# Emitting the conv of unit 20 and four weight tiles of the first down product inside the last up pair, and activation loads ahead of weight loads

## The chip, the cores and the metric

The kernel runs on one core of a Trainium2 chip. The metric is the device time of one execution in microseconds (us). A time without further words is the median of three runs; the profile is one execution more, with a time of its own.

## The reference, cut to what matters

One decoder layer: a mixer (retention and spatial gating), then a gated MLP with a causal depthwise convolution of width 3, then a last norm. The change lies wholly in the MLP, of which this is the computation (sequence 1024, model width 1024, inner width 2816, float32):

```
h = rmsnorm(x, ffn_norm_g[l])
up = causal_depthwise_conv(h @ w_up[l], conv_w[l], conv_b[l])
a, b = jnp.split(up, 2, axis=-1)
x = x + (jax.nn.silu(a) * b) @ w_down[l]
...
return rmsnorm(x, final_norm_g)
```

## The kernel before, in words

**Arithmetic.** Both matrix products of the MLP are done on 2x2 blocks with seven block products in place of eight (numbered 1 to 7). TensorE (PE) gets each float32 operand as two parts, a rounded one (h) and the rest (l): ScalarE (ACT) makes h by a copy, VectorE (DVE) makes l by a subtraction (`split_w`, L113 and L114, for weights; `load_act`, L809 and L810, for activations). Each block product then takes three matmuls for each pair of tiles: weight h with activation h, weight h with activation l, weight l with activation h. A matmul has 128 rows and 512 columns.

**Up units.** The inner width is cut into 22 tiles (FT = 22); one `Unit` computes a tile of both halves of the up product (`u20`, `u21` are the last two). Its steps on PE come in the order 1, 2, 5, 6, 3, 7, 4. Their weights: `a` and `d` are parts of the loaded tiles; `s` (split into `bh`, `bl`; steps 5 and 6) and `t` (split into `ch`, `cl`; steps 3 and 7) are sums of them, made on DVE in most units and, in the last pair, on GpSimd (POOL), L159. A unit's results `ra` and `rb` go to `conv`: `taps` for each of the two (ACT L756, DVE L757 and L758), a Silu (ACT L765) and the product of both (L767); the tiles are `cv20` and `cv42` for unit 20, `cv21` and `cv43` for unit 21. `blocks_of` then writes the products' activation blocks to memory (POOL: DMAs L774, L775, L778, L779 and subtractions L777), from where the down stage loads them.

**The last pair.** Unit 20 (`held`) is written out as the others, unit 21 (`last`) by `pair`, which calls a hook `ahead(1)` to `ahead(6)` between the steps; the hook emits first work of the down stage.

**The down stage.** Its seven products come in the order 2, 1, 5, 6, 3, 7, 4 (`SEQ`). A product has 4 output parts (p = 0 to 3) and 11 pairs of inner tiles, 33 matmuls for each part, 132 in all. Names: `wd20h` is the h part of weight tile 0 of product 2, with 8 of its 44 inner tiles, `g23l` the l part of activation tile 3 of product 2, with 2 of 11; so part p = 0 needs all activation tiles but of the weights only tiles 0 and 1. A product thus loads six weight tiles (512 KB each; two loads where two weights are summed) and six activation tiles (`g..`; the last of products 2 and 1 stays on chip as `g2e`, `g1e`). `dZ` are the sums of product 2 on PE, `dX` those of products 1, 6, 7 and 4, `dY` those of 5 and 3. `acc` (L855) adds finished sums to the output tiles `x2`.

**What sets the order.** The loads are issued by SyncE (SP), which works down its queue in order: a load that waits for its buffer holds all behind it. `PREP` is the list of a product's loads, and `prep(i, n)` emits the next n of product i. Raw up weights, their sums `s` and `t` and raw down weights share one pool of 4 tiles (`W`), so a load of a weight waits until the l part of the tile that had its place is made. The program's text does not fix the order on an engine: a scheduler sets it by due times and priorities as the text gives them, and each engine then works its own queue in order. In the down loop the order on PE is that of the text.

Of the kernel before, what the change touches and what calls it, by code (L numbers as in the profile page):

```python
# [13 lines left out]
ALU = mybir.AluOpType  # L14
# [9 lines left out]
FT = FF // P  # L24
# [41 lines left out]
def decoder_layer(ctx, tc, io, out):  # L66
    nc = tc.nc
# [8 lines left out]
    def U(name, dt=F32, shape=(P, 1024)):  # L76
        return up.tile(list(shape), dt, tag="u", name=name)
# [10 lines left out]
    def W(name):  # L88
        return wp.tile([P, 8, P], F32, tag="w", name=name, bufs=4)
# [16 lines left out]
    def split_w(src, name, tile=None, eng=None):  # L106
        n = src.shape[1]
        if tile:
            wh, wl = tile(name + "h"), tile(name + "l")
        else:  # L110
            wh = wp.tile([P, 8, P], F32R, tag="wh", name=name + "h")
            wl = wp.tile([P, 8, P], F32R, tag="wl", name=name + "l")
        nc.scalar.activation(wh[:, :n], src, AF.Copy)  # L113
        (eng or nc.vector).tensor_tensor(wl[:, :n], src, wh[:, :n].bitcast(F32), ALU.subtract)  # L114
        return wh, wl
# [35 lines left out]
    class Unit:  # L151
# [9 lines left out]
        def prep(u, src, key, eng=None):  # L161
            h, l = split_w(src, u.name + key, eng=eng)
            return [(h[:, o:o + u.kh], l[:, o:o + u.kh]) for o in range(0, src.shape[1], u.kh)]
# [105 lines left out]
    def unit(srcs, R, name):  # L269
        u = Unit(load_pair(srcs, name), R, name)  # L270
        u.prep_a()
        u.p(1)
        u.p(2)
        return finish(u)
# [479 lines left out]
    def taps(r, i):  # L754
        t = U(f"cv{i}")
        nc.scalar.activation(t, r, AF.Identity, scale=V("cw", 88 + i), bias=V("cb", i))  # L756
        nc.vector.scalar_tensor_tensor(t[:, 1:], r[:, :S - 1], V("cw", 44 + i), t[:, 1:], ALU.mult, ALU.add)  # L757
        nc.vector.scalar_tensor_tensor(t[:, 2:], r[:, :S - 2], V("cw", i), t[:, 2:], ALU.mult, ALU.add)  # L758
        return t
# [3 lines left out]
    def conv(ra, rb, i):  # L763
        a = taps(ra, i)
        nc.scalar.activation(a, a, AF.Silu)  # L765
        b = taps(rb, FT + i)
        (nc.gpsimd if i < 2 or i == FT - 2 else nc.vector).tensor_tensor(a, a, b, ALU.mult)  # L767
        g[i] = halves(a)


# [42 lines left out]
    def last_act(i, x):  # L813
        e = U(f"g{i}e", F32R, PAIR)
        nc.scalar.activation(e[:, 0], x, AF.Copy)
        nc.vector.tensor_tensor(e[:, 1], x, e[:, 0].bitcast(F32), ALU.subtract)
        act[i].append((e[:, 0], e[:, 1]))


    def load_wt(i, t):  # L820
        lo, n = 8 * t, min(8, NB - 8 * t)
        raw = []
        for m, src in enumerate(SRC[i]):
            raw.append(W(f"wd{i}{t}{m}")[:, :n])
            nc.sync.dma_start(raw[-1], src[:, lo:lo + n])
        w = raw[0]
        if i == 5:
            sums[t] = U(f"ds{t}", F32, (P, 8, P))
        if i in (5, 6, 3):
            s = sums[t][:, :n]  # L830
            x, y, op = {5: (w, raw[-1], ALU.add), 6: (s, w, ALU.subtract), 3: (w, s, ALU.subtract)}[i]
            nc.vector.tensor_tensor(s, x, y, op)  # L832
            w = s
        elif i == 7:
            nc.vector.tensor_tensor(w, w, raw[1], ALU.subtract)  # L835
        h, l = split_w(w, f"wd{i}{t}", tile=(lambda name: U(name, F32R, (P, 8, P))) if i == 2 and t % 2 == 0 or i == SEQ[-1] and t < 4 else None)
        wts[i] += [(h[:, m], l[:, m]) for m in range(n)]
# [3 lines left out]
    def load_x2(n):  # L841
        x2[n] = U(f"x2{n}")
        nc.sync.dma_start(x2[n], x2d[:, n])
# [12 lines left out]

    PREP = {2: [(load_act, j) for j in range(5)]}
    for i in SEQ[1:]:
        PREP[i] = [f for j in range(6) for f in ((load_act, j), (load_wt, j))]
        if i == 1:  # L860
            PREP[i] = [f for f in PREP[i] if f != (load_act, 5)]

# [6 lines left out]
    def pair(u, ahead):  # L869
        u.p(1)  # L870
        ahead(1)
        u.p(2)
        u.sums_s(nc.gpsimd)
        u.split_s()
        ahead(2)
        u.p(5)
        ahead(3)
        u.p(6)
        u.sums_t(nc.gpsimd)
        u.split_t()  # L880
        ahead(4)
        u.p(3)
        u.prep_b()
        ahead(5)
        u.p(7)
        ahead(6)
        u.p(4)

    for i, (ra, rb) in enumerate(early):
        conv(ra, rb, i)  # L890
    blocks_of(0)
    conv(*finish(u2), 2)
    for i in range(3, FT - 2):
        conv(*unit([io["w_up"][:, i], io["w_up"][:, FT + i]], R, f"u{i}"), i)
        if i % 2:
            blocks_of(i // 2)

    held = unit([io["w_up"][:, FT - 2], io["w_up"][:, 2 * FT - 2]], R, f"u{FT - 2}")
    last = Up(FT - 1)

    def ahead(j):
        if j in (1, 2, 3, 4, 5):
            prep(2, 1)
        if j == 4:
            load_wt(2, 0)
        if j == 5:
            load_wt(2, 1)
        if j == 6:
            prep(1, 1)

    pair(last, ahead)
    load_wt(2, 2)
    conv(*held, FT - 2)
    prep(1, 1)
    load_x2(0)
    load_x2(2)
    conv(last.ra, last.rb, FT - 1)
    e, o = g[FT - 2], g[FT - 1]
    last_act(2, o[:, 0])
    for t in range(3, 6):  # L920
        load_wt(2, t)
    last1 = U("g1e", F32R, PAIR)
    nc.scalar.activation(last1[:, 0], e[:, 0], AF.Copy)
    nc.vector.tensor_tensor(last1[:, 1], e[:, 0], last1[:, 0].bitcast(F32), ALU.subtract)
# [57 lines left out]
    with tc.manual_schedule(engines={mybir.EngineType.PE, mybir.EngineType.DVE, mybir.EngineType.Activation}):  # L982
# [8 lines left out]
        for k in range(8):  # L991
            s, p = divmod(k, 4)
            b = (bb, bc)[s]
# [54 lines left out]
```

## Time and profile before

| | before |
|---|---|
| median of 3 runs | 1091.77 us |
| lowest, highest | 1091.1, 1093.42 us |
| the profiled execution | 1095.39 us |
| its span on the core | 1093.6 us (so 1.8 us outside of it) |
| mean granted clock of TensorE | 0.978 |
| PE, DVE, ACT, POOL busy | 95%, 76%, 45%, 20% of the span |

Times in the rows are in us from the span's start. A row of a timeline gives the start, the duration, the engine, the line, what is written from what, and in brackets the idle time just before it with the instruction that ended it. Matmul durations overlap; their pitch, not their duration, says how fast PE goes. The last up unit ends and the down stage begins about 838 us after the start; product 4 ends just ahead of the end of the span.

### The profile page before, as it was taken

Reading aid. Unit: us, or ns where it says so; the run is one execution under the profiler, and the core shown is the slowest. Engines: PE = TensorE matmul, PEld = TensorE weight load, DVE = VectorE, ACT = ScalarE, POOL = GpSimd, SP = SyncE. Lnnn points to the kernel's source line nnn. Section 1 sums busy time; section 2 is a strip of 40 time slices with the busy share of each in tenths; the row PEclk is TensorE's granted clock in tenths of the full one; section 3 lists DMA queues with packets and bytes.
Section 4 is the critical chain, followed back from the end, with each engine's and each line's share of the span. In section 5 each row is a group of like instructions: output and inputs, shape, how many; then the busy total and the mean of one; then the engine's idle time right before and its main releaser. Section 6 shows DMA issues by size and latency. Waiting matters only on the chain.

```text
span 1093.6 us, 12687 instructions
## 1 busy us (share of the span) xinstructions
PE 1039.0 (95%) x4786; PEld 854.1 (78%) x4786; DVE 831.5 (76%) x990; ACT 492.3 (45%) x691; POOL 223.3 (20%) x152
## 2 busy tenths in 40 slices
PE   7798999999999997989999999999999979999986
PEld 5576888888888885778888888888887757888886
DVE  6967886968787398798887878788787747876655
ACT  6663434344455253553444544454454423344430
POOL 4502230513110006052223032122322210000000
PEclk9998999999999998999999999999999989999998
DMA  7251031212274240023333133232327568972514
GB/s 280 78 193 39 22 109 59 71 57 79 78 251 173 77 173 1 20 87 106 106 116 108 67 125 116 84 109 103 105 82 259 201 222 308 355 253 104 189 62 154
DMA packets 48445, 141.57 MB, mean 129 GB/s; under 512 B 5056, under 2 KB 9536, under 8 KB 48384
## 3 DMA queue, kind: packets, MB, share of 16 engines
q1 hardware_dynamic: 42752, 120.58, 31.8%
q0 software_dynamic: 5632, 20.19, 4.8%
q8 instruction: 37, 0.61, 0.2%
q14 instruction: 24, 0.20, 0.1%
HBM read 109.03 MB, written 31.72 MB: 129 GB/s over the span
## 4 chain that ended last, share of the span: by engine, by line
PE 67%; DVE 15%; issue 5%; DMA 4%; ACT 3%; POOL 1%; SPq 0%; DVEq 0%; ACTq 0%
PE dX L850 8%; PE po L135 8%; PE dY L850 5%; DVE cv L758 2%; DVE cv L757 1%; PE A2X L146 1%; PE G1X L146 1%; DMA g13l<-gb 1%; PE A3X L146 1%; PE B3X L146 1%; PE B1X L146 1%; PE u20X L146 1%; PE u0X L146 1%; PE G2X L146 1%; PE G3X L146 1%
## 5 line engine op out<-in xcount | busy, mean ns | idle before, releaser
L765 ACT ACTIVATE cv<-cv 128x1024 f32<-128x1024 f32 x22 | 23.4, 1062 | 71.8 <-DVE cv L758 71.8
L777 POOL TENSOR_TENSOR cv<-cv 128x512 f32<-128x512 f32 x22 | 38.4, 1745 | 22.1 <-DMA gb<-cv 16.5
L775 POOL DMA_DIRECT2D gb<-cv x11 | 7.9, 714 | 123.4 <-DVE cv L767 123.1
L777 POOL TENSOR_TENSOR cv<-cv,cv 128x512 f32<-128x512 f32 x22 | 29.6, 1346 | 4.2 <-DMA gb<-cv 2.4
L774 POOL DMA_DIRECT2D gb<-cv x11 | 6.5, 591 | 101.7 <-DVE cv L767 101.1
L936 ACT ACTIVATE x3q<-x 128x256 f32<-128x256 f32 (+1 forms) x21 | 9.4, 481 | 38.7 <-DVE x L997 30.2
L652 DVE TENSOR_TENSOR xr<-po,xr 128x512 f32<-128x512 f32 x16 | 10.9, 689 | 20.3 <-PE po L135 20.3
L675 POOL TENSOR_TENSOR nx<-nx,rsb 128x1024 f32<-128x1024 f32 x2 | 5.7, 2893 | 93.6 <-ACT rsb L719 93.6
L767 POOL TENSOR_TENSOR cv<-cv,cv 128x1024 f32<-128x1024 f32 x3 | 9.8, 3271 | 66.0 <-DVE cv L758 64.8
L767 DVE TENSOR_TENSOR cv<-cv,cv 128x1024 f32<-128x1024 f32 x19 | 23.1, 1217 | 0.1
L658 ACT ACTIVATE xq<-xr 128x512 f32<-128x512 f32 x14 | 8.8, 626 | 22.2 <-DVE xr L652 15.2
L546 ACT ACTIVATE sT<-po 128x128 f32<-128x128 f32 x32 | 8.4, 277 | 13.3 <-PE po L538 13.2
L832 DVE TENSOR_TENSOR ds<-wd,wd 128x1024 f32<-128x1024 f32 (+1 forms) x6 | 6.8, 1133 | 9.0 <-DMA wd<-in_w_down 9.0
L835 DVE TENSOR_TENSOR wd<-wd,wd 128x1024 f32<-128x1024 f32 (+1 forms) x6 | 6.8, 1135 | 8.6 <-DMA wd<-in_w_down 8.6
L284 POOL TENSOR_TENSOR nx<-nx,nx 128x1024 f32<-128x1024 f32 x4 | 12.3, 3093 | 3.5 <-DVE nx L729 3.5
L938 DVE TENSOR_TENSOR sq<-sq,x3q 128x256 f32<-128x256 f32 (+1 forms) x20 | 9.8, 517 | 4.2 <-ACT x3q L936 3.8
L947 DVE SCALAR_TENSOR_TENSOR x<-x,vec,r 128x256 f32<-128x256 f32 (+1 forms) x24 | 12.0, 565 | 0.8 <-PE r L619 0.8
L662 DVE TENSOR_TENSOR sq<-sq,xq 128x512 f32<-128x512 f32 x14 | 9.6, 688 | 2.5 <-ACT xq L658 2.3
L997 DVE TENSOR_TENSOR x<-dX,x 128x256 f32<-128x256 f32 x8 | 3.4, 424 | 9.8 <-PE dX L850 9.8
L672 ACT ACTIVATE nx<-xr,vec 128x512 f32<-128x512 f32 x16 | 10.8, 708 | 0.0
L509 ACT ACTIVATE kn<-pk,vec 128x512 f32<-128x512 f32 x8 | 5.2, 679 | 11.8 <-PE pk L508 11.8
L336 POOL TENSOR_SCALAR x<-x,vec 128x512 f32<-128x512 f32 x4 | 8.5, 2128 | 6.7 <-DVE R110l L330 6.7
(5707 smaller groups left out, 3893.5 us busy)
## 6 DMA issues: line engine op xcount, KB each, us to landing
wd<-in_w_down SPq DMA_DIRECT2D x45, 512.0 KB, 4.4
gb<-cv POOLq DMA_DIRECT2D x33, 512.0 KB, 3.2
wo<-in_w_out SPq DMA_DIRECT2D x10, 512.0 KB, 3.9
x<-in_xT SPq DMA_DIRECT2D x8, 512.0 KB, 9.2
xn<-in_xN SPq DMA_DIRECT2D x8, 512.0 KB, 6.0
xr<-in_xT SPq DMA_DIRECT2D x8, 512.0 KB, 6.1
x2d<-xr SPq DMA_DIRECT2D x8, 512.0 KB, 3.1
x<-x2d SPq DMA_DIRECT2D x8, 512.0 KB, 6.1
```

Of the source, the lines that this page charges most:

```text
L135: nc.tensor.matmul(ps, a, b, start=(k == 0 and t == 0), stop=(k == n - 1 and t == 2))
L146: nc.tensor.matmul(ps, a[:, k], b, start=(start and i == 0), stop=(i == 3 * n - 1), skip_group_check=not start)
L284: eng.tensor_tensor(o[j], a[j], b[j], ALU.subtract)
L652: nc.vector.tensor_tensor(u.y, u.ps, u.y, ALU.add)
L672: nc.scalar.activation(nx[n // 2][:, n % 2], xr[th][n // 2][:, n % 2], AF.Identity, scale=V("g2", n))
L757: nc.vector.scalar_tensor_tensor(t[:, 1:], r[:, :S - 1], V("cw", 44 + i), t[:, 1:], ALU.mult, ALU.add)
L758: nc.vector.scalar_tensor_tensor(t[:, 2:], r[:, :S - 2], V("cw", i), t[:, 2:], ALU.mult, ALU.add)
L765: nc.scalar.activation(a, a, AF.Silu)
L767: (nc.gpsimd if i < 2 or i == FT - 2 else nc.vector).tensor_tensor(a, a, b, ALU.mult)
L777: nc.gpsimd.tensor_tensor(x, y, z, ALU.subtract)
L850: nc.tensor.matmul(ps, w[s // 2], r[s % 2][:, cols], start=first, stop=stop and n == len(todo) - 1, skip_group_check=True)
L947: nc.vector.scalar_tensor_tensor(y, y, V("gf", n), u.nr.rs, ALU.mult, ALU.mult)
```

## The change

Three edits. First, the product L767 of unit 20's conv goes from POOL to DVE. Second, `PREP` of every product but the first is no longer activation and weight in turn, but activations 0 and 1, weight 0, activations 2 and 3, weight 1, activations 4 and 5, weight 2, then weights 3, 4 and 5. Third, the hooks: unit 20's conv is emitted at `ahead(1)`, inside the last pair, in place of behind it; the weight tiles 0 to 3 of product 2 are emitted at `ahead(3)` to `ahead(6)` (before: 0 and 1 at `ahead(4)` and `ahead(5)`, 2 behind the pair, 3 to 5 behind unit 21's conv); all six stand ahead of unit 21's conv, and product 1's first loads come only behind them.

```diff
-        (nc.gpsimd if i < 2 or i == FT - 2 else nc.vector).tensor_tensor(a, a, b, ALU.mult)
+        (nc.gpsimd if i < 2 else nc.vector).tensor_tensor(a, a, b, ALU.mult)
...
-        PREP[i] = [f for j in range(6) for f in ((load_act, j), (load_wt, j))]
+        PREP[i] = [(f, int(j)) for f, j in zip([load_act, load_act, load_wt] * 3 + [load_wt] * 3, "010231452345")]
...
     def ahead(j):
-        if j in (1, 2, 3, 4, 5):
+        if j == 1:
+            conv(*held, FT - 2)
+        if j < 6:
             prep(2, 1)
-        if j == 4:
-            load_wt(2, 0)
-        if j == 5:
-            load_wt(2, 1)
-        if j == 6:
-            prep(1, 1)
+        if j > 2:
+            load_wt(2, j - 3)
 
     pair(last, ahead)
-    load_wt(2, 2)
-    conv(*held, FT - 2)
-    prep(1, 1)
+    for t in range(4, 6):
+        load_wt(2, t)
+    prep(1, 2)
+    conv(last.ra, last.rb, FT - 1)
     load_x2(0)
     load_x2(2)
-    conv(last.ra, last.rb, FT - 1)
     e, o = g[FT - 2], g[FT - 1]
     last_act(2, o[:, 0])
-    for t in range(3, 6):
-        load_wt(2, t)
```

What this makes of the queues is seen at three places. On DVE, behind the l part of unit 21's `s`, there stood before:

```order
L114 TENSOR_TENSOR u21bl_6189<-u21s_6185,u21bh_6188 128x1024
L159 TENSOR_TENSOR u21ra_6183<-u21Z_6170,u21p1_6163 128x512
L114 TENSOR_TENSOR u21cl_6235<-u21t_6231,u21ch_6234 128x1024
L810 TENSOR_TENSOR g20l_6166<-g20l_6166,g20h_6165 128x1024
L114 TENSOR_TENSOR u21dl_6263<-u21w1_6143,u21dh_6262 128x512
L810 TENSOR_TENSOR g21l_6193<-g21l_6193,g21h_6192 128x1024
L114 TENSOR_TENSOR wd21l_6274<-wd210_6271,wd21h_6273 128x1024
L810 TENSOR_TENSOR g22l_6213<-g22l_6213,g22h_6212 128x1024
L159 TENSOR_TENSOR u21ra_6183<-u21Y_6197,u21p6_6229 128x512
L810 TENSOR_TENSOR g23l_6239<-g23l_6239,g23h_6238 128x1024
L114 TENSOR_TENSOR wd20l_6246<-wd200_6243,wd20h_6245 128x1024
```

and there stands now:

```order
L757 SCALAR_TENSOR_TENSOR cv20_6165<-u20ra_6053,vec_75,cv20_6165 128x1023
L758 SCALAR_TENSOR_TENSOR cv20_6165<-u20ra_6053,vec_75,cv20_6165 128x1022
L757 SCALAR_TENSOR_TENSOR cv42_6170<-u20rb_6123,vec_75,cv42_6170 128x1023
L159 TENSOR_TENSOR u21ra_6193<-u21Z_6180,u21p1_6163 128x512
L758 SCALAR_TENSOR_TENSOR cv42_6170<-u20rb_6123,vec_75,cv42_6170 128x1022
L810 TENSOR_TENSOR g20l_6176<-g20l_6176,g20h_6175 128x1024
L767 TENSOR_TENSOR cv20_6165<-cv20_6165,cv42_6170 128x1024
L810 TENSOR_TENSOR g21l_6203<-g21l_6203,g21h_6202 128x1024
L810 TENSOR_TENSOR g22l_6223<-g22l_6223,g22h_6222 128x1024
L114 TENSOR_TENSOR wd20l_6230<-wd200_6227,wd20h_6229 128x1024
L810 TENSOR_TENSOR g23l_6255<-g23l_6255,g23h_6254 128x1024
L114 TENSOR_TENSOR u21cl_6251<-u21t_6247,u21ch_6250 128x1024
```

Four tap instructions of unit 20's conv and its L767 have come in ahead of the activation parts, and `u21cl`, which stood third, stands last.

On POOL, behind the sum `u21s`, there stood before (`u21t` is the sum that `u21ch` and `u21cl` are split from, `gb` the blocks in memory):

```order
L159 TENSOR_TENSOR u21t_6231<-u21w0_6142,u21s_6185 128x512
L159 TENSOR_TENSOR u21t_6231<-u21w0_6142,u21w1_6143 128x512
L775 DMA gb10_3523<-cv19_5999 128x2x512
L777 TENSOR_TENSOR cv18_5864<-cv19_5999,cv18_5864 128x512
L778 DMA gb10_3523<-cv18_5864 128x2x512
L777 TENSOR_TENSOR cv19_5999<-cv19_5999,cv18_5864 128x512
L777 TENSOR_TENSOR cv19_5999<-cv19_5999 128x512
L779 DMA gb10_3523<-cv19_5999 128x2x512
L767 TENSOR_TENSOR cv20_6315<-cv20_6315,cv42_6320 128x1024
L774 DMA gb1_3524<-cv20_6315 128x512
```

and there stands now:

```order
L775 DMA gb10_3523<-cv19_5999 128x2x512
L777 TENSOR_TENSOR cv18_5864<-cv19_5999,cv18_5864 128x512
L778 DMA gb10_3523<-cv18_5864 128x2x512
L777 TENSOR_TENSOR cv19_5999<-cv19_5999,cv18_5864 128x512
L777 TENSOR_TENSOR cv19_5999<-cv19_5999 128x512
L779 DMA gb10_3523<-cv19_5999 128x2x512
L774 DMA gb1_3524<-cv20_6165 128x512
L159 TENSOR_TENSOR u21t_6247<-u21w0_6142,u21s_6195 128x512
L159 TENSOR_TENSOR u21t_6247<-u21w0_6142,u21w1_6143 128x512
```

The pair that makes `u21t` has moved behind the blocks of units 18 and 19 and the first DMA of unit 20's, and the L767 is gone. In the changed program `u21t` also waits for `wd20l`, whose raw weight has its place in the pool. On PE, the first 16 matmuls of `dZ` (g20 to g23 with `wd20h`) thereby stand ahead of unit 21's step 3, which needs `u21ch`; before, they stood behind its step 7.

On SP, from product 2's first weight on, there stood before:

```order
L825 DMA wd200_6243<-in_w_down 128x1024
L808 DMA g20l_6166<-gb10_3523 128x1024
L825 DMA wd210_6271<-in_w_down 128x1024
L808 DMA g21l_6193<-gb10_3523 128x1024
L825 DMA wd220_6309<-in_w_down 128x1024
L808 DMA g22l_6213<-gb10_3523 128x1024
L825 DMA wd100_6325<-in_w_down 128x1024
L808 DMA g23l_6239<-gb10_3523 128x1024
L825 DMA wd230_6348<-in_w_down 128x1024
L808 DMA g24l_6267<-gb10_3523 128x1024
L825 DMA wd240_6354<-in_w_down 128x1024
```

and there stands now:

```order
L825 DMA wd200_6227<-in_w_down 128x1024
L808 DMA g20l_6176<-gb10_3523 128x1024
L808 DMA g21l_6203<-gb10_3523 128x1024
L808 DMA g22l_6223<-gb10_3523 128x1024
L808 DMA g23l_6255<-gb10_3523 128x1024
L808 DMA g24l_6283<-gb10_3523 128x1024
L825 DMA wd210_6259<-in_w_down 128x1024
L825 DMA wd220_6287<-in_w_down 128x1024
L825 DMA wd230_6307<-in_w_down 128x1024
L825 DMA wd240_6326<-in_w_down 128x1024
L825 DMA wd250_6332<-in_w_down 128x512
```

The activations of product 2 are issued in a row, and product 1's first weight stands behind all six of product 2.

## Rows read from the trace of the kernel before

**Rows 1.** The page: busy time, share of the span, instructions of each engine.

```profile
PE 1039.0 (95%) x4786; PEld 854.1 (78%) x4786; DVE 831.5 (76%) x990; ACT 492.3 (45%) x691; POOL 223.3 (20%) x152
```

**Rows 2.** The chain that ended last: start us, us, what (xcount).

```profile
873.12 10.96 DMA g13l<-gb
...
891.47 28.40 PE dX L850 x115
...
925.96 27.98 PE dY L850 x115
953.95 29.92 PE dX L850 x132
...
1061.71 4.05 PE dX L850 x33
```

**Rows 3.** Timeline of PE in the down stage, at starts of products and at waits.

```profile
837.96 0.39 PE L146 MATMUL u21Y<-R220h,u21ch 128*128 128x512 f32 x1
...
869.69 0.50 PE L850 MATMUL dZ<-g20h,wd24h 128*128 128x512 f32 x1 [2.25 <-ACT wd24h L113]
...
879.35 0.39 PE L850 MATMUL dX<-g10h,wd10h 128*128 128x512 f32 x1
...
885.21 0.54 PE L850 MATMUL dX<-g13h,wd10h 128*128 128x512 f32 x1 [2.97 <-ACT g13h L809]
...
890.21 0.80 PE L850 MATMUL dX<-g14h,wd11h 128*128 128x512 f32 x1 [2.09 <-ACT g14h L809]
...
919.69 0.39 PE L850 MATMUL dY<-g50h,wd50h 128*128 128x512 f32 x1
...
925.96 0.50 PE L850 MATMUL dY<-g54l,wd51h 128*128 128x512 f32 x1 [1.64 <-DVE g54l L810]
...
1043.54 0.28 PE L850 MATMUL dX<-g40h,wd40h 128*128 128x256 f32 x1
...
1049.32 0.56 PE L850 MATMUL dX<-g44l,wd41h 128*128 128x256 f32 x1 [2.45 <-DVE g44l L810]
...
1052.85 0.28 PE L850 MATMUL dX<-g40h,wd41h 128*128 128x256 f32 x1
```

**Rows 4.** Timelines of ACT, DVE and POOL, about the last up pair.

```profile
834.54 0.60 ACT L246 ACTIVATE u20rb<-u20X 128x512 f32<-128x512 f32 x1 [0.27 <-PE u20X L146]
...
842.91 1.04 ACT L113 ACTIVATE wd20h<-wd 128x1024 fp32r<-128x1024 f32 x1
854.80 1.23 ACT L756 ACTIVATE cv<-u20rb,vec 128x1024 f32<-128x1024 f32 x1
...
843.04 1.23 DVE L810 TENSOR_TENSOR g23l<-g23l,g23h 128x1024 fp32r<-128x1024 f32 x1 [0.69 <-ACT g23h L809]
856.13 1.28 DVE L757 SCALAR_TENSOR_TENSOR cv<-u20rb,vec,cv 128x1023 f32<-128x1023 f32 x1
859.71 1.27 DVE L758 SCALAR_TENSOR_TENSOR cv<-u20rb,vec,cv 128x1022 f32<-128x1022 f32 x1
862.10 3.41 DVE L758 SCALAR_TENSOR_TENSOR cv<-u21ra,vec,cv 128x1022 f32<-128x1022 f32 x1
866.81 1.23 DVE L767 TENSOR_TENSOR cv<-cv,cv 128x1024 f32<-128x1024 f32 x1
...
817.14 1.29 POOL L159 TENSOR_TENSOR u21t<-u21w,u21s 128x512 f32<-128x512 f32 x1 [0.68 <-DVE u20dl L114]
818.39 2.28 POOL L159 TENSOR_TENSOR u21t<-u21w,u21w 128x512 f32<-128x512 f32 x1
861.17 3.26 POOL L767 TENSOR_TENSOR cv<-cv,cv 128x1024 f32<-128x1024 f32 x1 [28.38 <-DVE cv L758]
```

**Rows 5.** Stretches: us, busy of PE, PEld, DVE, ACT, POOL; granted clock, DMA share, GB/s.

```profile
892.00:894.00 2.00, 2.00 (x6) 1.55 (x5) 0.55 (x1) 0.00 (x0) 0.00 (x0) 0.50 0.00 0
```

**Rows 6.** Timeline of SP: issues of three late activation loads.

```profile
882.81 0.43 SPq L808 DMA_DIRECT2D g14l<-gb  x1
...
916.42 0.42 SPq L808 DMA_DIRECT2D g54l<-gb  x1
...
1024.71 0.42 SPq L808 DMA_DIRECT2D g41l<-gb  x1
```

## The prediction

> **What bounds the kernel now.** I read the page first: PE is busy 95% of the span and DVE 76% [rows 1], so a gain can only be time that PE loses, and it has to be looked for where the change works, from the last up unit on. The chain of waits there runs through PE but for single loads and their splits [rows 2]. It also gives a pitch: 132 matmuls in 29.92 us, 0.2267 us each [rows 2]. Against it I set the starts in PE's timeline [rows 3], stage by stage:
>
> A, from the last unit's step 3 to product 1: 837.96 to 879.35 is 41.39 us for 168 matmuls (36 of the unit, 120 + 12 of product 2), worth 38.08: 3.3 lost, of it 2.25 for `wd24h`.
> B, product 1: 879.35 to 919.69 is 40.34, worth 29.92: 10.4 lost. The rows show 2.97 for `g13h` and 2.09 for `g14h`; the load of g13 alone took 10.96 us [rows 2].
> C, product 5: 919.69 to 953.95 is 34.26: 4.3 lost, of it 1.64 for `g54l`.
> D, the first quarter of product 4: 1043.54 to 1052.85 is 9.31, worth 4.05 by a later quarter [rows 2]: 5.3 lost, 2.45 for `g44l`.
>
> Together 23.3 us. The waits named are less than that, since PE also runs slowly after a wait: at 892 to 894 it was busy throughout at a granted clock of 0.50, the lower of its two levels, 1.2 GHz [rows 5]; it had waited just before. The price of such a restart is in the chain: behind the wait for g14 115 matmuls took 28.40 us where the pitch gives 26.07, so 2.3 lost, and behind the wait for g54 27.98, so 1.9 [rows 2]. I use 2.
>
> **The change part by part. The front, A.** This is where the change costs. The order puts 16 matmuls of `dZ` ahead of the unit's step 3 on PE, four for each of g20 to g23, and unit 20's conv ahead of these activations on DVE. The conv waits for `u20rb`, which ACT ends at 835.1 [rows 4]; DVE and ACT work their queues in order, so nothing passes it. From there I walk DVE's queue with the durations of [rows 4], less a tenth where instructions overlap: ACT's tap 1.2, to 836.3; L757 on `cv42`, to 837.5; half of `u21ra` 0.6; L758, to 839.3; `g20l`, 1.1 (its 1.23 holds a little overlap), to 840.4; L767, now on DVE at 1.23, to 841.6; `g21l` 842.7, `g22l` 843.9, `wd20l` 845.0, `g23l` 846.2. PE, free at 838.0, gets its first four matmuls about when `wd20h` and `g20l` are there, 841.7 at the latest, and the last four of the 16 at 846.2.
>
> Then comes the second wait. POOL's `u21t` waits for `wd20l`, 845.0, because the one takes the other's place in the pool; its two instructions took 1.29 and 2.28 [rows 4], so it ends at 848.9; ACT's split of a weight tile takes 1.04 [rows 4], `u21ch` the same: PE goes on at 850.1. Between 838.0 and 850.1 it does 16 matmuls, 3.6 us, and waits 8.5. With 2 for the restart the new A loses 10.5. Queued behind `u21t` on POOL is only a DMA of unit 21's conv, which nobody needs yet; queued behind `u21ch` on ACT is `g24h`, which is late by the same and needed after `u21ch`. The old loss of A goes: all splits of product 2's weights are now emitted ahead of unit 21's conv, and the conv of unit 20, five DVE instructions of some 1.2 us, no longer stands at 855 to 866 between the loads and the splits.
>
> *Bounds of the front.* The trace of before has neither wait. Below: if the bursts are hidden better and the clock holds, the waits to 841.7 alone with a short one for `u21ch`, 5 us. Above: the clock stays low until the unit's last step, a rival below. I take 10.5, by the walk through rows that exist one by one. The Trainium skill (GPSIMD Engine Reference, 1. Specifications) says that POOL shares its SBUF interfaces with VectorE and is disturbed by VectorE instructions with two operands from SBUF. The rows with `u21t` (1.29 and 2.28) and with DVE's L758 beside POOL's L767 (3.41 in place of 1.27) [rows 4] bear this out; by it both halves of `u21t` might take 2.28 beside DVE's splits, and the sum below would be a gain 1 us smaller.
>
> Moving L767 from POOL (3.26) to DVE (1.23) [rows 4] costs DVE 1.2 us that stand in the walk; it takes away the disturbed L758, 3.41 for 1.27. Off POOL it frees nothing that is waited for.
>
> **B.** Product 1 now begins at 837.96 + 38.08 + 10.5 = 886.5 in place of 879.35. g13 is issued ahead of wd14, well before it is needed, and no longer among three weights: its 2.97 goes. g14 stands behind wd14, which waits for `wd10l`, and DVE makes that one behind unit 21's conv: by the same walk about 877 to 878. So g14 is issued near 880 (882.81 before [rows 6]); its h part was there at 890.2 and the l part takes 1.23 more, 8.6 us after the issue, so it is ready near 888.5; product 1 wants it 16 matmuls after its start, at 890.2. It is a near thing; I put 1.2 for it. Gain 9.2.
>
> **C.** In the new list g54 stands behind two weight tiles of product 5 in place of four, each of two loads. It was issued at 916.42 [rows 6] and made PE wait 1.64; with four loads fewer ahead it is there in time, though product 5 begins earlier by 2 us (919.7 + 7.2 − 9.2). Gain 4.3.
>
> **D.** g41 was issued at 1024.71 [rows 6], behind weights that waited for places; in the new order it stands right behind g40, and g43 and g44 stand two weights earlier. g44l was 2.45 late and comes earlier by more. Gain 5.3. Products 6, 3 and 7 lose nothing now; the weights that slip back there (tile 1 by two places) are wanted 16 matmuls into a product at the earliest, tile 2 in its second quarter.
>
> **Sum.** 23.3 lost before, 10.5 + 1.2 after: 11.6 us gained. On the profiled execution (span 1093.6, 1.8 outside, 1095.39) that is 1083.8; it ran 3.6 above the median, so the median goes from 1091.77 to 1080.2.
>
> **The rivals.**
> *Half of the tail stays.* C or D keeps its loss, because the load is late for its buffer and not for its place in the list: about 5 less, 1085. For it: I could not resolve each wait of SP there. Against it: g54 and g41 stood behind weights.
> *g14 late again.* If g14 is issued after 884, B costs what it did: 9.2 less, 1089.4. It decides on `wd10l`, which hangs on unit 21's conv.
> *The clock stays low.* PE works in bursts of four between 838 and 850. If the lower level holds for the 59 matmuls from there to the end of the unit's last step, each costs 0.2267 more, 13.4 in place of 2: 11.4 less, 1091.6, no change. For it is the slow stretch at 892, behind waits; against it that the restart there lost but 2.3 us, ten matmuls' worth. The Trainium skill (TensorE: Matmul & The Clock Gate, HAM oscillation) says that an engine that keeps waiting between short groups of matmuls is throttled again and again, which speaks against breaking up this stretch; the stretch at 892 agrees for one wait, and no row shows a series of them.
> *Slower: lateness is handed on.* Buffers are freed by PE and DVE, which are 7.2 us late after the front (10.5 − 3.3). If the loads of all later products are paced by these buffers and not by the list, each comes late by the same, and B, C and D keep their losses: 7.2 us slower, 1099.0. It decides in product 1: g14 issued after 884 and again a wait in product 5. Against it: g54 was held by its place in the queue.
> *No effect.* The front's waits are filled by other work and the reordered lists change nothing: 1091.8.
>
> **How the numbers follow.** Forecast 0.55; half of the tail 0.15; g14 late 0.10; clock low 0.07; no effect 0.04; slower 0.09. A measurement of this kernel tells some 0.2%, 2.2 us, from no change. Faster: 0.55 + 0.15 + 0.10 = 0.80; within 0.2%: 0.11; slower: 0.09. The range has the first three: its low end is the forecast with the front at 5 (5.5 less, 1074.7, say 1075.0), its high end the late g14 with 1 us more for `u21t`, 1090.5; 0.20 is left out.
>
> **What would show it.** Right: PE waits at some 838 to 842 before the first `dZ` and again until about 850 for `u21ch`, with POOL's `u21t` at 845 to 849; no wait for `wd24h`; product 1 starting near 886 and lasting about 31; product 5 without a wait for `g54l`; product 4 without one for `g44l`. Wrong: a second or third wait between 850 and 865 (for `wd21l` or g24), a granted clock near 0.5 through that stretch, or waits for weight tiles 1 or 2 where activations were waited for.

## The result, and the profile after

The changed kernel takes 1084.36 us (median of six runs, 1082.13 to 1087.84), the kernel before 1093.36 in six runs (1091.1 to 1093.58), 9.0 us less. Every ratio in this document is one of averages, not of medians: here 0.9926, 95% interval 0.9905 to 0.9948, which is 8.1 us less. A second set of six, beside eleven of before, gave 1085.72 against 1093.4, 0.9914 (0.9887 to 0.9941). The forecast was 11.6 us less with a range of 1075.0 to 1090.5: the sign and the range hold, and one term was missing.

The profiled execution took 1087.08 us (span 1085.3). On the page the sums hardly move: PE 1039.0 to 1036.6, DVE 831.5 to 830.0 (for [rows 1]).

```profile
PE 1036.6 (96%) x4786; PEld 854.6 (79%) x4786; DVE 830.0 (76%) x991; ACT 492.1 (45%) x691; POOL 225.2 (21%) x151
```

What moved is seen only by stage. The waits of PE between 836 and 1075 us in the kernel after (engine, line and tile that waited, and for what; us in total, times, longest):

```profile
PE dZ L850 <- ACT wd20h L113: 3.5, 1, 3.5
PE u21Y L146 <- ACT u21ch L113: 2.5, 1, 2.5
PE dX L850 <- DVE g65e L810: 2.3, 1, 2.3
PE dX L850 <- DVE g64l L810: 0.8, 1, 0.8
PE dX L850 <- DVE g14l L810: 0.5, 1, 0.5
```

Of the five waits in [rows 3] (`wd24h`, `g13h`, `g14h`, `g54l`, `g44l`) only half a microsecond for g14 is left. Two new ones stand in front, and two in product 6, where before there was none. PE's timeline of the kernel after, at the places that answer to [rows 3]:

```profile
837.76 0.50 PE L850 MATMUL dZ<-g20h,wd20h 128*128 128x512 f32 x1 [3.52 <-ACT wd20h L113]
...
845.96 0.80 PE L146 MATMUL u21Y<-R220h,u21ch 128*128 128x512 f32 x1 [2.49 <-ACT u21ch L113]
...
883.42 0.39 PE L850 MATMUL dX<-g10h,wd10h 128*128 128x512 f32 x1
...
887.94 0.50 PE L850 MATMUL dX<-g14l,wd11h 128*128 128x512 f32 x1 [0.50 <-DVE g14l L810]
...
914.16 0.39 PE L850 MATMUL dY<-g50h,wd50h 128*128 128x512 f32 x1
...
944.08 0.39 PE L850 MATMUL dX<-g60h,wd60h 128*128 128x512 f32 x1
...
952.39 0.79 PE L850 MATMUL dX<-g65e,wd61h 128*128 128x512 f32 x1 [2.28 <-DVE g65e L810]
...
980.30 0.39 PE L850 MATMUL dY<-g30h,wd30h 128*128 128x512 f32 x1
...
1040.14 0.28 PE L850 MATMUL dX<-g40h,wd40h 128*128 128x256 f32 x1
```

The starts of the products give their lengths. The table has them for all profiled executions: A runs from the start of the last two matmuls of unit 21's step 6, one row in the timeline, to product 1 (before: 837.51 to 879.35), the next columns from a product's first matmul to the next one's, product 4 to the last start of its first tile `g40h`. Products 3 and 7 took 29.9 in every one. The last column is the ratio to the runs of the kernel before that were made beside it.

| profiled execution | start of A | A | product 1 | product 5 | product 6 | product 4 | A to end | ratio of the averages |
|---|---|---|---|---|---|---|---|---|
| before | 837.5 | 41.8 | 40.3 | 34.1 | 29.9 | 38.4 | 256.1 | 1 |
| after | 833.6 | 49.8 | 30.7 | 29.9 | 36.2 | 33.1 | 251.7 | 0.9926 |
| after, again | 834.7 | 46.9 | 31.5 | 29.9 | 36.6 | 33.1 | 249.8 | 0.9914 |
| list only | 833.6 | 42.2 | 36.1 | 29.9 | 31.7 | 33.1 | 244.4 | 0.9906 |
| hooks only | 833.2 | 46.9 | 33.3 | 34.0 | 29.9 | 37.6 | 253.2 | 0.9967 |
| weights a hook later | 833.4 | 47.0 | 29.9 | 29.9 | 31.7 | 33.1 | 243.8 | 0.9919 |
| x2 first | 834.1 | 48.2 | 30.5 | 29.9 | 32.4 | 33.1 | 245.5 | 0.9937 |
| conv behind | 838.0 | 42.8 | 33.4 | 30.3 | 33.2 | 33.1 | 244.3 | 0.9902 |
| weights later, conv behind | 833.8 | 40.6 | 39.6 | 30.1 | 36.3 | 33.1 | 251.6 | 0.9942 |
| product on POOL | 833.2 | 49.6 | 31.8 | 29.9 | 35.0 | 33.1 | 251.3 | 0.9918 |
| odd x2 in product 1 | 835.9 | 46.9 | 30.4 | 30.1 | 35.3 | 33.1 | 247.8 | 0.9910 |
| conv behind, t apart, x2 | 833.2 | 40.7 | 35.0 | 30.4 | 35.3 | 33.1 | 245.9 | 0.9905 |
| list only, x2 | 835.6 | 45.0 | 36.2 | 29.9 | 32.2 | 33.1 | 248.0 | 0.9903 |
| second tile in the other pool | 835.3 | 49.8 | 30.8 | 30.5 | 31.0 | 33.1 | 246.6 | 0.9907 |

Two things must be read with it. The start of A differs by up to 4.8 us between executions. The edits are not the reason: from unit 3's first matmul to unit 21's it took 349.5 to 349.8 us in every execution, and the difference is there already at unit 3 (472.16 before, 468.11 after), ahead of all that was edited. So a difference of whole times between two profiled executions is no measure, and 3.9 of the 8.3 us between before and after stand there. And the runs of one kernel spread: those of conv behind reach from 1076.85 to 1089.84. The intervals of all ratios are 0.003 to 0.006 wide. They tell no kernel of the table but the one before from after; hooks only comes nearest (0.9947 at its lower end, where after's two sets end at 0.9948 and 0.9941), and it is slower than list only, which ends at 0.993. The stage lengths carry the conclusions below; the medians only bound them.

### The profile page after: what moved, and what is told of

Same layout as the page of the kernel before. It is cut to its first block, busy times and chain, and to the rows that moved or that the text cites. A ratio compares the mean times of both kernels' runs of the same rounds, so it can differ in the third digit from the quotient of the medians.

```text
span 1085.3 us, 12687 instructions
## 1 busy us (share of the span) xinstructions
PE 1036.6 (96%) x4786; PEld 854.6 (79%) x4786; DVE 830.0 (76%) x991; ACT 492.1 (45%) x691; POOL 225.2 (21%) x151
## 4 chain that ended last, share of the span: by engine, by line
PE 76%; DVE 14%; issue 5%; ACT 3%; DMA 1%; POOL 1%; SPq 0%; DVEq 0%; ACTq 0%
PE dX L850 10%; PE po L135 8%; PE dY L850 5%; PE dZ L850 2%; DVE cv L758 2%; PE A0X L146 2%; PE B0X L146 1%; DVE cv L757 1%; PE A2X L146 1%; PE G1X L146 1%; PE A3X L146 1%; PE B3X L146 1%; PE u20X L146 1%; PE u12X L146 1%; PE G0X L146 1%
## 5 line engine op out<-in xcount | busy, mean ns | idle before, releaser
L765 ACT ACTIVATE cv<-cv 128x1024 f32<-128x1024 f32 x22 | 23.4, 1063 | 72.4 <-DVE cv L758 72.4
L777 POOL TENSOR_TENSOR cv<-cv,cv 128x512 f32<-128x512 f32 x22 | 31.5, 1434 | 5.8 <-DMA gb<-cv 4.5
L767 DVE TENSOR_TENSOR cv<-cv,cv 128x1024 f32<-128x1024 f32 x20 | 24.3, 1216 | 0.1
L658 ACT ACTIVATE xq<-xr 128x512 f32<-128x512 f32 x14 | 8.8, 627 | 22.1 <-DVE xr L652 15.1
L767 POOL TENSOR_TENSOR cv<-cv,cv 128x1024 f32<-128x1024 f32 x2 | 6.6, 3280 | 36.0 <-DVE cv L758 34.8
L675 DVE TENSOR_TENSOR nx<-nx,r 128x1024 f32<-128x1024 f32 x6 | 7.0, 1215 | 3.5 <-ACT rsb L719 3.1
```

The lines of the kernel that those rows point to most:

```text
L675: eng.tensor_tensor(t, t, rs.unsqueeze(1).to_broadcast(list(PAIR)), ALU.mult)
L767: (nc.gpsimd if i < 2 else nc.vector).tensor_tensor(a, a, b, ALU.mult)
L777: nc.gpsimd.tensor_tensor(x, y, z, ALU.subtract)
```

## The experiments

**The list alone, and the hooks alone.** First, which part of the change buys what. The list alone is the kernel before with this edit:

```diff
-        PREP[i] = [f for j in range(6) for f in ((load_act, j), (load_wt, j))]
+        PREP[i] = [(f, int(j)) for f, j in zip([load_act, load_act, load_wt] * 3 + [load_wt] * 3, "010231452345")]
```

> The kernel before with the new order of loads in PREP alone (hooks, conv and its product as before). Theory: the front cost of the change (stage A: 41.4 us before, 49.2 after) comes from the hooks, and the gains of product 1 (40.3 to 30.8), product 5 (34.3 to 29.9) and product 4's first quarter from the list. Then A stays near 41, product 1 takes about 31, product 5 about 30, product 6 about 36 (its new wait comes with the list too), product 4 about 33: 12 to 13 us below before, a ratio of 0.988. Rival: product 1's gain comes from the hooks, which load product 2's weights earlier; then product 1 stays at 40 and only 3 us are gained, 0.997.

It measured 1080.51 against 1091.3, 0.9906 (0.9883 to 0.993). Products 5 and 4 are as in after, so their gains are the list's. A stays at 42.2, so the front's cost is the hooks'. Product 1 took 36.1: 4.2 of its 9.6 us. Neither the theory (31) nor the rival (40) holds. Product 6 took 31.7, not the 36 that was expected. Its longest waits from 825 to 1075 us:

```profile
PE dX L850 <- ACT g14h L809: 2.4, 1, 2.4
PE dZ L850 <- ACT wd24h L113: 2.1, 1, 2.1
PE dX L850 <- DVE g65e L810: 1.5, 1, 1.5
```

g13 is in time, g14 is not, and `wd24h` stalls PE as before, since product 2's last weights still stand behind the convs.

The hooks alone are the changed kernel with the reverse edit:

```diff
-        PREP[i] = [(f, int(j)) for f, j in zip([load_act, load_act, load_wt] * 3 + [load_wt] * 3, "010231452345")]
+        PREP[i] = [f for j in range(6) for f in ((load_act, j), (load_wt, j))]
```

> The changed kernel with the old order of loads in PREP (hooks, conv and its product as changed). Theory: A takes 49 us as after, product 1 about 40, product 5 about 34, product 6 30 and product 4 as before: 7 to 8 us above before, a ratio of 1.007. Rival (product 1's gain comes from the hooks): A 49, product 1 31, 1 to 2 us below before, 0.9985.

It measured 1087.7, 0.9967 (0.9947 to 0.9987), on the rival's side of no change. Product 1 took 33.3, so the hooks too give 7.0 of its 9.6 us; products 5 and 4 keep their losses, and product 6 has none. The longest waits, but for the 3.5 for `wd20h` that after has too:

```profile
PE dX L850 <- DVE g14l L810: 3.1, 1, 3.1
PE u21Y L146 <- ACT u21ch L113: 2.5, 1, 2.5
PE dX L850 <- DVE g44l L810: 2.0, 1, 2.0
PE dY L850 <- DVE g54l L810: 2.0, 1, 2.0
```

So product 1 gains from either part, and from both no more than what there is to be had (30.7, where no wait would be 29.9).

**What costs the front its 8 us.** Two things come in ahead of unit 21's step 3: unit 20's conv on DVE and ACT, and weight 0 of product 2, which takes the place in the pool that `u21t` wants. Weights a hook later undoes the second, with the conv left inside the pair:

```diff
-        if j > 2:
-            load_wt(2, j - 3)
+        if j > 3:
+            load_wt(2, j - 4)
...
-    for t in range(4, 6):
+    for t in range(3, 6):
         load_wt(2, t)
```

> The changed kernel with product 2's weight tiles emitted one hook later (0 to 2 in ahead(4) to ahead(6), 3 to 5 behind the pair); unit 20's conv stays inside the pair. On POOL u21t then stands right behind u21s again and on PE the unit's step 3 ahead of dZ. Theory: the front cost is that weight tile 0 takes the place in the pool that u21t needs, so A falls from 49 to 41 or 42 and the kernel is 7 to 8 us faster than after: 0.985 of before. Rival: the cost is unit 20's conv, which stands on DVE ahead of the activation splits and waits for u20rb; it still does, so PE waits for g20l to g23l and A stays at 46 to 49: 0.990 to 0.992.

It measured 1082.71, 0.9919 (0.9902 to 0.9936). The wait for `u21ch` is gone, but A took 47.0: the rival holds. The chain of waits (start us, us, what) and the row of PE show by which way the conv still costs:

```profile
835.74 1.27 DVE cv L758
837.01 1.15 DVE wd21l L114
838.16 0.02 issue
838.18 0.33 SPq L825
...
838.68 4.36 DMA g23l<-gb
...
844.03 1.05 ACT wd20h L113
```

```profile
845.12 0.80 PE L850 MATMUL dZ<-g20h,wd20h 128*128 128x512 f32 x1 [4.80 <-ACT wd20h L113]
```

A tap stands on DVE ahead of `wd21l`; only that split frees the place for the next weight on SP; g23 stands on SP behind this weight; and on ACT `wd20h` stands behind `g23h`. Product 1 had no wait here: g14 was issued at 859.43, ahead of weight 4, not behind it.

The counterpart leaves the weights early and moves the conv out of the pair:

```diff
     def ahead(j):
-        if j == 1:
-            conv(*held, FT - 2)
...
     for t in range(4, 6):
         load_wt(2, t)
+    conv(*held, FT - 2)
     prep(1, 2)
```

> The changed kernel with unit 20's conv out of the last pair, behind it, after product 2's six weights and ahead of product 1's first loads; the weights stay at ahead(3) to ahead(6), so weight 0 still takes the place that u21t needs and dZ stands ahead of the unit's step 3. If the conv on DVE is the cost of the front, PE no longer waits 3.5 us for wd20h and A falls by 4 to 6, to 44 to 46: 4 to 6 us faster than after. If the place in the pool is the cost, the wait for u21ch stays or grows, and A stays at 48 to 50.

A fell to 42.8, and the wait for `u21ch` to 1.3: the conv is the larger part of the front's cost, 4 to 7 us, and the place in the pool a small one. It measured 1082.34, 0.9902 (0.9871 to 0.9933); product 1 gave 2 to 3 us back, with a wait of 2.1 for `g14h`.

Both together:

```diff
-        if j == 1:
-            conv(*held, FT - 2)
...
-        if j > 2:
-            load_wt(2, j - 3)
+        if j > 3:
+            load_wt(2, j - 4)
...
-    for t in range(4, 6):
+    for t in range(3, 6):
         load_wt(2, t)
     prep(1, 2)
+    conv(*held, FT - 2)
```

> The changed kernel with both: product 2's weights a hook later and unit 20's conv behind the pair, behind all of product 2's weights and product 1's first two loads. Theory: the two parts of the hooks cost by two paths, each enough by itself (with the weights early u21t waits for their place; with the conv early the weight and activation splits stand behind its taps); only without both does A fall to 41 to 43, and product 1 keeps most of its gain (31 to 34), since product 2's weights still stand ahead of the convs: 0.982 to 0.985 of before. Rival: product 1's gain hangs on unit 20's conv being early; then product 1 takes 36 or more and the ratio is 0.988 to 0.990 as with the list alone.

The front is healed, 40.6, and nothing is won by it: product 1 took 39.6, product 6 36.3, and the ratio is 0.9942 (0.9926 to 0.9957), the highest among the kernels that have both edits in some form. The theory's 0.982 to 0.985 fell; the rival's 36 or more for product 1 holds, but its 0.988 to 0.990 was still too low:

```profile
PE dX L850 <- DVE g13l L810: 3.2, 1, 3.2
PE dX L850 <- DVE g65e L810: 2.3, 1, 2.3
PE dX L850 <- ACT g14h L809: 2.1, 1, 2.1
```

SP waited 16.7 us for the place of `wd10l`, which DVE made among the instructions of both convs (865.54). g13 stood behind that wait and was issued at 867.77, and g14 at 876.62, behind weight 4 and two tiles of x2, with PE 8.9 us earlier at product 1 (874.48 against 883.42). What the front gives is taken back at the next late load.

**The product's engine.** The first edit of the change undone:

```diff
-        (nc.gpsimd if i < 2 else nc.vector).tensor_tensor(a, a, b, ALU.mult)
+        (nc.gpsimd if i < 2 or i == FT - 2 else nc.vector).tensor_tensor(a, a, b, ALU.mult)
```

> The changed kernel with the product L767 of unit 20's conv back on POOL (3.3 us there, 1.2 on DVE). On POOL it then stands ahead of u21t, on DVE the splits g21l to g23l come 1.1 us earlier. Theory: u21t waits for wd20l in any case and then for the longer POOL queue; PE's wait for u21ch stays within 1 us, and the time within 2 us of after. Rival: POOL's product is disturbed by DVE and ends after wd20l; then u21ch is 2 to 3 us later, and the kernel that much slower than after.

It measured 1084.36, 0.9918 (0.9904 to 0.9932), A 49.6 and the wait for `u21ch` 2.5 as in the first profile of after. The theory holds; this part of the change is worth nothing that can be measured.

**Product 6's new loss.** The first suspect was the load of x2 behind the weights on SP, with DVE's queue behind the addition that waits for it. In after:

```profile
934.43 5.47 SPq L825 DMA_DIRECT2D wd<-in_w_down  x2
939.95 0.42 SPq L843 DMA_DIRECT2D x<-x2d  x1
940.48 0.37 SPq L808 DMA_DIRECT2D g64l<-gb  x1
```

```profile
944.77 0.69 DVE L855 TENSOR_TENSOR x<-dY,x 128x512 f32<-128x512 f32 x1 [1.23 <-DMA x<-x2d]
945.38 1.22 DVE L114 TENSOR_TENSOR wd61l<-ds,wd61h 128x1024 fp32r<-128x1024 f32 x1
946.51 1.22 DVE L114 TENSOR_TENSOR wd62l<-ds,wd62h 128x1024 fp32r<-128x1024 f32 x1
947.65 1.22 DVE L810 TENSOR_TENSOR g64l<-g64l,g64h 128x1024 fp32r<-128x1024 f32 x1
```

The load of x2 ahead of each hook's loads:

```diff
+                if i == 5:
+                    load_x2(2 * p + 1)
                 prep(nxt, 3)
...
-                    if i == 5:
-                        load_x2(2 * p + 1)
```

> The changed kernel with the loads of x2 in product 5 emitted ahead of the three loads of each hook, not behind them. Theory: product 6's new loss (29.9 us before, 36.2 after) is that the load of x2 stands on SP behind weights that wait for places, and DVE's queue behind the addition that waits for it; then product 6 takes 30 to 32 and the kernel is 4 to 6 us faster than after: 0.988 of before. Rival: product 6 waits for g65e's own load, issued late in the new list; then it stays at 35 to 36, and the ratio at 0.992.

Product 6 took 32.4, near what the theory says, but the ratio stayed at 0.9937 (0.9917 to 0.9957). Weights a hook later had 31.7 with the loads of x2 where after has them. So this run does not show that it is x2; the next three tested it further. First the kernel after itself once more:

> The changed kernel itself once more, beside the others of this call. In its first profile product 6 took 36.2 us with a wait of 2.3 for g65e; with the same list of loads and no edit there, the run with the weights a hook later showed 31.7. Theory now: the long product 6 belongs to that one execution, a load of x2 that landed late; then it takes 31 to 33 here, stage A 49 to 50, product 1 31, the median about 0.992 of before. Rival: it belongs to the changed order of the front; then 35 to 36 again.

36.6: the long product 6 belongs to the changed kernel and not to one execution, as the rival says. It takes both parts of the change: 31.7 with the list alone, 29.9 with the hooks alone. Then the odd x2 tiles far earlier:

```diff
                     if i == 1:
+                        load_x2(2 * p + 1)
                         X[p] = A(f"dX{p}")
...
-                    if i == 5:
-                        load_x2(2 * p + 1)
```

> The changed kernel with the four odd x2 tiles (512 KB each) loaded from product 1's hooks, not product 5's; on SP they then stand among product 5's loads, 8 to 20 places earlier. Theory: product 6's loss (5 to 7 us in the profiles of after, none before) is what product 5's loss was, handed on: between 30 us ahead of product 6 and its start the loads of product 5's two-tile weights, the activations and x2 fill the DMA engines, so with no wait in product 5 the activations of product 6 are issued later by PE's clock (g64 at 26 us after product 5's start, 22 before). Earlier there is room on the DMA engines; with the x2 tiles there, g64 is issued by 22 or 23 and product 6 takes 30 to 32: 4 to 5 us faster than after. Rival: the loads are paced by places in the pool for weights all along; then x2 costs no time where it stands and product 6 stays at 35 to 37, or the wait moves to product 5 (g53, g54) for the same sum.

Product 6 took 35.3, as the rival says, with waits of 1.7 for `g64l` and 1.5 for `g64h`. Taking x2 away does not shorten it; but the wait is another one than in after, none is left for `g65e`, and g64 was issued 28.4 us after product 5's start. So it is not shown that the place of x2 makes no difference. The ratio is 0.9910 (0.9885 to 0.9935). Last, the second raw tile of each of product 5's sums out of the pool of 4:

```diff
-            raw.append(W(f"wd{i}{t}{m}")[:, :n])
+            raw.append((UW if i == 5 and m else W)(f"wd{i}{t}{m}")[:, :n])
```

> The changed kernel with the second raw weight tile of each of product 5's sums in the larger pool (38 tiles) instead of the pool of 4, so that product 5's loads need half the places there; the same bytes are loaded. Where the loads of x2 stood made no difference to product 6. Theory: it is the places in the pool of 4, freed one by one by DVE's sums and splits, that pace SP through product 5 (SP stood at two weight loads for 5.5 us just ahead of g64 in after); with more of them g64 is issued by 22 to 23 us after product 5's start and product 6 takes 30 to 32, 4 to 5 us faster than after. Rival: the DMA engines pace it (busy 0.9 of the time between 900 and 950); then product 5 and 6 together stay at 65 to 67 us, whichever of them shows the wait.

Product 6 took 31.0, products 5 and 6 together 61.5, where after had 66.1 and 66.6. The same bytes were loaded, so the rival of the DMA engines, 65 to 67 for both products, falls. The theory's route is only half right: g64 was issued 25.0 us after product 5's start (915.8), not 22 to 23, against 26.3 in after. The edit also changed the order on DVE, where `g64l` now stood ahead of `wd62l`. How much is due to the places and how much to this order is not shown. What is left of the waits of products 5 and 6, among those from 825 to 1060 us:

```profile
PE dX L850 <- DVE g65e L810: 0.8, 1, 0.8
...
PE dY L850 <- DVE x L855: 0.2, 1, 0.2
```

The ratio is 0.9907 (0.9889 to 0.9924): 5 us less in product 6 of one execution, and a ratio that can't be told from after's.

**Two attempts at a faster version.** The first is conv behind and odd x2 in product 1 (their edits above) with `u21t` in a tile of the larger pool (`sums_t` gets the tile as an argument); the second is the list alone with the edit of odd x2 in product 1. The one new edit:

```diff
-        u.sums_t(nc.gpsimd)
+        u.sums_t(nc.gpsimd, UW)
```

> The changed kernel with unit 20's conv behind the pair (as in the run conv behind), u21t in a tile of the other pool so that weight 0 of product 2 takes no place from it, and the odd x2 loaded from product 1's hooks. Theory: the first removes the wait for wd20h, the second that for u21ch and lets SP go on with product 2's weights 15 us earlier, the third product 6's wait: A 41 to 43, product 1 30 to 34, product 5 30, product 6 30 to 32: 0.978 to 0.982 of before, the fastest so far. Rival: what the front gives is handed on to product 1, since its loads hang on the places that free up behind both convs: A 42, product 1 36 to 38, 0.985 to 0.988.

A took 40.7 as expected, but product 1 35.0 and product 6 35.3: 1082.74, 0.9905 (0.9883 to 0.9928). The front's gain was handed on, as the rival says, and beyond product 1 to product 6, so that the time is above what either gave.

> The kernel before with the new list and the odd x2 loaded from product 1's hooks, hooks as before. Theory: product 6 as before (30), product 1 as with the list alone (36), A 42 to 43: 1 to 2 us faster than the list alone, 0.988 to 0.990 of before. Rival: the x2 loads crowd out g13 and g14 of product 1; then product 1 goes to 38 or more and nothing is gained on the list alone.

1083.08, 0.9903 (0.9882 to 0.9923): product 1 as with the list alone, 36.2, product 6 32.2, not the 30 expected, A longer (45.0, with waits of 2.4 for `wd24h` and 1.2 for `wd20h`), nothing gained. No version here is shown to beat the changed kernel, although the list alone has 5 to 7 us less from A to the end in its profile than after in its two. Nor are the hooks shown to add anything to the list: the list alone stands at 0.9906, the whole change at 0.9926 and 0.9914.

## Why the prediction was right, and where it was short

**The front (predicted 10.5 lost in A, 7.2 more than before): right in size.** A is 8.0 longer in the first profile of after and 5.1 in the second. The walk along DVE's queue came out nearly to the instruction. The start of A is 3.9 us earlier here, so the predicted 841.7 for the first `dZ` is 837.8, and it is at 837.76; the end of `u21t`, predicted at 848.9 − 3.9 = 845.0, is at 844.82, and step 3, predicted at 846.2, at 845.96. The queue in the timelines of DVE, POOL and ACT of after:

```profile
840.09 1.22 DVE L114 TENSOR_TENSOR wd20l<-wd,wd20h 128x1024 fp32r<-128x1024 f32 x1
841.40 2.19 POOL L159 TENSOR_TENSOR u21t<-u21w,u21s 128x512 f32<-128x512 f32 x1 [2.62 <-DVE wd20l L114]
843.56 1.26 POOL L159 TENSOR_TENSOR u21t<-u21w,u21w 128x512 f32<-128x512 f32 x1
844.85 1.06 ACT L113 ACTIVATE u21ch<-u21t 128x1024 fp32r<-128x1024 f32 x1 [6.19 <-POOL u21t L159]
```

The two halves of `u21t` took 2.19 and 1.26, together 3.45 where [rows 4] gave 3.57, and not 2.28 twice. The split between waits and clock was off: 6.0 of waits, not 8.5, and about 5 of slow matmuls, not 2. That the sum comes near, 11.3 for 10.5, is in part luck: the two misses have opposite signs. The windows of after show it (us, busy of PE, PEld, DVE, ACT, POOL, granted clock, DMA share, GB/s):

```profile
840.00:842.00 2.00, 2.00 (x7) 1.57 (x6) 2.00 (x3) 0.00 (x0) 0.60 (x1) 0.52 0.01 2
...
848.00:850.00 2.00, 2.00 (x7) 1.52 (x6) 2.00 (x3) 1.28 (x3) 0.00 (x0) 0.50 0.84 246
850.00:852.00 2.00, 2.00 (x6) 1.61 (x5) 1.28 (x2) 0.49 (x1) 0.00 (x0) 0.50 0.75 203
```

At the clock's lower level the 16 matmuls of `dZ` took 5.7 us (837.76 to 843.47) in place of 3.6, and the 24 behind `u21ch` 8.6 (845.96 to 854.57) in place of 5.4. There were two restarts to pay, not one, because there were two waits. The rival of a clock that stays low through all 59 matmuls came about only in part: some 5 of its 13.4 us were lost, and the clock was back at 1.00 from 854 on. The Trainium skill (TensorE: Matmul & The Clock Gate, HAM oscillation) tells of a kernel in which the wait for a load between short groups of matmuls throttles the engine anew at every group; here the trace agrees, with two slow stretches behind the waits of 3.52 and 2.49. Not every wait of that size did it: behind the 2.25 for `wd24h` in the trace of before [rows 3] the clock stood at 1.00.

```profile
871.00:873.00 2.00, 2.00 (x10) 1.65 (x9) 1.89 (x3) 0.11 (x1) 1.16 (x1) 1.00 0.93 277
```

One thing the runs add: I put the cost down to the conv and the place in the pool in one sum. Conv behind shows that the conv is most of it.

**Product 1 (predicted 9.2 gained): right,** 9.6 and 8.8. g14 was the near thing that I took it for: issued at 877.40 (predicted near 880, less 3.9), and PE waited 0.50 (predicted 1.2). But the text gave the gain to the list, which brings g13 ahead of weight 4; the two runs with one part each show that the list gives 4.2 and the hooks 7.0 by themselves.

**Product 5 (4.3) and product 4 (5.3): right,** 4.2 and 5.3 in every kernel with the list (product 5 within 0.5), and still lost with the hooks alone.

**Products 6, 3 and 7 (predicted to lose nothing): wrong for product 6.** This is the term that was missing, 6.3 and 6.7 us: in the first profile 3.1 of waits and 3.2 of slow matmuls behind them. With it the sum 11.6 becomes about 5, which is what the profiles show from A to the end: 256.1 before, 251.7 and 249.8 after. I had argued that only the weights slip back in the new list and that they are wanted late. What I did not weigh is that product 6's own loads are emitted while product 5 runs: PE came to product 6 4.2 us sooner after product 5's start, while g64 was issued 4.3 us later after it, 22.1 before (941.75) and 26.3 in after. It stands behind weights that wait for places in the pool of 4, and product 5 uses two places for each weight tile. It is the rival of lateness handed on, at one product only.

Nor did I walk DVE's queue there, where the new list sets another order. Before, `g64l` stood ahead of two weights' splits and `g65e` right behind them:

```profile
950.36 1.22 DVE L810 TENSOR_TENSOR g64l<-g64l,g64h 128x1024 fp32r<-128x1024 f32 x1
...
953.15 1.23 DVE L114 TENSOR_TENSOR wd61l<-ds,wd61h 128x1024 fp32r<-128x1024 f32 x1 [0.97 <-ACT g65e L809]
954.29 1.22 DVE L114 TENSOR_TENSOR wd62l<-ds,wd62h 128x1024 fp32r<-128x1024 f32 x1
955.42 0.69 DVE L810 TENSOR_TENSOR g65e<-g65e 128x512 fp32r<-128x512 f32 x1
```

In after `g64l` stands behind both (the DVE rows at 944.77 to 947.65 above), and `g65e` behind two sums of weights (`ds`) besides. The chain that ended last runs through this queue, from the load of x2 on:

```profile
939.95 4.80 DMA x<-x2d
...
949.47 2.27 DVE ds L832 x2
951.74 0.61 DVE g65e L810
...
952.39 7.67 PE dX L850 x21
```

The list alone has the same order on DVE. There the wait for x2 ended 1.6 us ahead of product 6's start (940.24 against 941.87), in after 0.7 behind it (944.77 against 944.08), and the loss was 1.8 against 6.3.

In the profiles without an edit to x2 or to product 5's tiles, the loss of product 6 goes roughly with how late g64 is issued after product 5's start: 0 at 22.0 to 22.1 (before and hooks only), 1.8 at 23.4 (weights a hook later), 1.8 at 24.0 (list only), 5.1 at 24.7 (product on POOL), 6.3 to 6.7 at 26.3 to 26.7 (after twice; weights later, conv behind). Conv behind, 3.3 at 26.5, does not fit, nor does second tile in the other pool, 1.1 at 25.0; so the issue is not all of it. How much the order on DVE costs by itself, no run isolates.

**What stays open.** The medians moved by 8 to 9 us, the stretch from A to the end by 4.5 to 6.3 in the profiles. There is one profile of before alone, and the start of A varies by up to 4.8 us for reasons that lie outside of the change, so I can't say whether the rest, 4.5 and 1.4 us, is chance of these executions; the lower ends of the two intervals are 5.7 and 6.4 us. By the stages alone the forecast of 11.6 would have been about twice too large, so that the median came as near to it as it did is in part not explained. Nor is it settled why g64 is issued 2.3 us sooner in list only than in after, with the same list: their fronts differ, and after's SP issued nothing between 827.80 and 843.62, where it waited 15.4 us for POOL's `u21t` and its place, so that more stood to be loaded behind it; but no run isolates that.

## What to carry to other kernels

Where PE waits at several loads in a row, a better order of loads takes each wait away by itself, but the next load that comes late can then show: count for each product when its loads can be issued by the buffers they need, and walk the queue of the engine that splits them, not only the queue of the loads. An operation moved ahead "into the shadow" of another stands in strict queues of two or three engines; walk the queue from the last thing that it must wait for, and the start of the delayed work can come out to within half a microsecond, as it did here. A gain of one stage in one profile says little until the sum over the following stages is taken.

## What the runs showed of the hardware

DVE's splits, 1.22 us alone, took about 2.3 us in stretches where POOL subtracted from one tile to another; in after, while POOL was busy 4.84 of the 5 us from 875 to 880:

```profile
875.80 2.31 DVE L810 TENSOR_TENSOR g12l<-g12l,g12h 128x1024 fp32r<-128x1024 f32 x1
878.03 2.31 DVE L810 TENSOR_TENSOR g13l<-g13l,g13h 128x1024 fp32r<-128x1024 f32 x1
```

```profile
875.00:880.00 5.00, 5.00 (x23) 4.13 (x23) 5.00 (x3) 0.84 (x1) 4.84 (x3) 1.00 0.67 229
```

So `blocks_of` on POOL, whose result is wanted later, slows splits that product 1 is about to need; PE did not wait for these two here. The Trainium skill (GPSIMD Engine Reference, 1. Specifications) says that the two engines contend for their interfaces to SBUF when a VectorE instruction reads two operands there; this row agrees, and the price here is nearly a factor of two for both splits. For the range I had priced the contention on POOL's side, in `u21t`, and not for these splits.
